# The S5 scan on VectorE alone with real and imaginary state tiles, and short convolutions on padded rows, in a hybrid S5 / SSD / DeltaNet step

## The chip, the core and the metric

The kernel runs on one NeuronCore of a Trainium2 chip. Five engines work side by side: TensorE (PE, with its weight loads shown as PEld), VectorE (DVE), ScalarE (ACT), GpSimd (POOL) and SyncE (SP), which here issues the transfers. Each engine runs its own instructions in a fixed order and waits on semaphores for the others. The metric is the device time of one execution in microseconds; smaller is better.

## What is computed

One layer of an inference step over T = 384 tokens, of which 128 are context and 256 latent (four grid rows of 64). The layer is a SwiGLU block, a mixer with three branches, and a second SwiGLU block; the change is in the mixer.

```python
u_s5, z, xbc, dt_raw, qkv, ... = jnp.split(h @ p['w_in'], IN_SPLITS, axis=-1)
# S5, diagonal complex recurrence, 32 groups x 64 states, forward and backward
y_f, ... = _s5_scan(u, ...);  y_b, ... = _s5_scan(_rev(u), ...)      # h_t = lb * h_{t-1} + B u_t
# short depthwise convolution of width 3, before SSD and DeltaNet
xbc = silu(_short_conv(xbc, ssd_conv_w, grid) + ssd_conv_b)
qkv = silu(_short_conv(qkv, dn_conv_w, grid))
# in _short_conv: context is one sequence of 128 tokens, latent rows are 64 tokens with zero ends
y = xp[:, :, 0:width] * w[0] + xp[:, :, 1:1+width] * w[1] + xp[:, :, 2:2+width] * w[2]
out = (sigmoid(gates) * branches).sum() @ w_out
```

## The kernel before

Tokens lie along the free axis, channels on the 128 partitions. Every dense product is made of three fp32r matmuls (`mm3`, L288): high part of the weight by high part of the input (L291), high by low (L292), low by high (L293). A block of 128 output channels gets its weights in `split_w` (L279): SP transfers 128x1024 numbers to `wraw` (three buffers, L281), ScalarE rounds them to `whi` (L284), VectorE subtracts to `wlo` (L285); `whi` and `wlo` have two buffers. So ScalarE and VectorE both stand between a transfer and TensorE, once for each block, in the order of their own queues.

The mixer comes at about 340 to 620 us. Its order of work is: four blocks of S5 input, the small scalars, twelve convolved blocks for k, q and v (L782 to L793; each q block also starts two `chunk_inputs`, L764, which copy a product from PSUM into the S5 state tile), the S5 scan (L806 to L822), four convolved x blocks, B and C (L830 to L836), the z blocks (L861 to L873), the decay masks (`segments`, L840: POOL makes `Atri`, TensorE sums it, ScalarE takes the exponential), the DeltaNet matrices and their inverse, and the S5 output matmuls (L967), which read the entering states `Hc`.

The order in which an engine's instructions stand is not the order of the source: a scheduler of the framework simulates the program and lays each engine's queue from its own estimates. So conv steps, scan steps and weight splits are interleaved in VectorE's queue, and TensorE's queue mixes z, segments, S5 outputs and further dense blocks.

**The scan.** Each chunk of 8 tokens is one step for 48 chunks; context (16 chunks) and the first half of the latent chain run abreast, so 31 steps do it: 15 of them with two columns (`nx` = 2) and 16 with one. The states are in `Ss[q]`, one tile for 16 of the 32 groups, with real and imaginary part inside. In a step each half takes two products (L818), a sum (L820) and an addition into the state (L822); half 0 is on VectorE, half 1 on GpSimd. When both halves are done ScalarE copies them, shifted by one chunk, into `Hc[q]` (L941 to L943), and GpSimd fills the start columns (L946, L947).

**The convolution** (`conv`, L662, called 18 times). ScalarE copies the block from PSUM to `ur` (L667), VectorE makes the middle tap (L671) and adds two side taps, each in one piece for context (127 columns, L677) and one for latent (4 rows of 63, L679); ScalarE applies SiLU (L681).

## Time and profile before

| | us |
|---|---|
| median of three runs | 1169.02 |
| lowest and highest of them | 1168.38, 1170.4 |
| the profiled execution | 1170.72 |
| its span in the trace | 1168.9 |

| engine | busy in the span |
|---|---|
| PE | 94% |
| PEld | 89% |
| DVE | 69% |
| ACT | 39% |
| POOL | 17% |

TensorE is busy nearly all the time, and its granted clock is 0.974 on average. The shares are averages over the whole span; in the mixer they are different, and the rows below are taken from there. A row of the stages gives the length of a stretch, then the busy time of each engine with its number of instructions, then the granted TensorE clock (1.00 is 2.4 GHz, 0.5 is 1.2 GHz), the DMA share and the bandwidth. A row by line gives line, engine, operation, what is written from what with the shapes, how often, busy time and mean duration, and the idle time of the engine before these instructions with what ended it.

### The profile page before, as it was taken

Reading aid. Unit: us, or ns where it says so; the run is one execution under the profiler, and the core shown is the slowest. Engines: PE = TensorE matmul, PEld = TensorE weight load, DVE = VectorE, ACT = ScalarE, POOL = GpSimd, SP = SyncE. Lnnn points to the kernel's source line nnn. Section 1 sums busy time; section 2 is a strip of 40 time slices with the busy share of each in tenths; the row PEclk is TensorE's granted clock in tenths of the full one; section 3 lists DMA queues with packets and bytes.
Section 4 is the critical chain, followed back from the end, with each engine's and each line's share of the span. In section 5 each row is a group of like instructions: output and inputs, shape, how many; then the busy total and the mean of one; then the engine's idle time right before and its main releaser. Section 6 shows DMA issues by size and latency. Waiting matters only on the chain.

```text
span 1168.9 us, 19259 instructions
## 1 busy us (share of the span) xinstructions
PE 1104.1 (94%) x7264; PEld 1039.9 (89%) x7264; DVE 807.4 (69%) x1698; ACT 458.0 (39%) x774; POOL 200.3 (17%) x270
## 2 busy tenths in 40 slices
...
GB/s 355 266 265 213 224 212 234 167 167 161 225 167 145 123 164 112 75 124 245 207 138 216 153 120 125 130 201 163 226 195 145 201 130 122 142 126 127 104 124 80
DMA packets 107342, 199.21 MB, mean 170 GB/s; under 512 B 35056, under 2 KB 61936, under 8 KB 106992
## 3 DMA queue, kind: packets, MB, share of 16 engines
...
q14 instruction: 37, 0.30, 0.1%
...
## 4 chain that ended last, share of the span: by engine, by line
PE 75%; DVE 12%; DMA 4%; issue 3%; ACT 3%; POOL 2%; SPq 1%; DVEq 0%; ACTq 0%; POOLq 0%
PE ps_d L293 20%; PE ps_d L291 20%; PE ps_d L292 20%; DVE wlo L285 2%; ACT whi L284 1%; DVE sc L818 1%; DMA wraw<-in_win_dram 1%; PE ps_c L1032 1%; PE ps_d L243 1%; PE ps_s L770 1%; PE ps_m L221 1%; PE ps_s L1032 1%; PE ps_m L849 1%; DVE cv L679 1%; DVE Ss L822 1%
## 5 line engine op out<-in xcount | busy, mean ns | idle before, releaser
L284 ACT CAST whi<-wraw 128x1024 fp32r<-128x1024 f32 (+3 forms) x247 | 227.9, 924 | 466.9 <-PE ps_d L292 306.4
L285 DVE TENSOR_TENSOR wlo<-wraw,whi 128x1024 fp32r<-128x1024 f32 (+3 forms) x247 | 276.3, 1119 | 120.8 <-ACT whi L284 119.7
L291 PE MATMUL ps_d<-hh,whi 128*128 128x384 f32 x696 | 243.1, 350 | 16.2 <-ACT whi L284 13.2
L293 PE MATMUL ps_d<-hh,wlo 128*128 128x384 f32 x696 | 243.7, 351 | 5.5 <-DVE wlo L285 5.4
L292 PE MATMUL ps_d<-hl,whi 128*128 128x384 f32 x696 | 242.2, 348 | 0.6 <-DVE hl L379 0.6
L291 PEld LDWEIGHTS ps_d<-hh,whi 128*128 128x128 f32 x696 | 134.4, 193 | 25.9 <-ACT whi L284 16.8
L293 PEld LDWEIGHTS ps_d<-hh,wlo 128*128 128x128 f32 x696 | 135.0, 194 | 12.8 <-DVE wlo L285 9.7
L292 PEld LDWEIGHTS ps_d<-hl,whi 128*128 128x128 f32 x696 | 135.1, 194 | 3.3 <-issue 1.8
L291 PE MATMUL ps_d<-xh,whi 128*128 128x386 f32 x352 | 120.0, 341 | 0.0
L293 PE MATMUL ps_d<-gh,wlo 128*128 128x384 f32 x352 | 119.1, 338 | 1.0 <-DVE wlo L285 1.0
L293 PE MATMUL ps_d<-xh,wlo 128*128 128x386 f32 x352 | 119.9, 341 | 0.0
L291 PE MATMUL ps_d<-gh,whi 128*128 128x384 f32 x352 | 118.8, 337 | 0.4 <-ACT whi L284 0.4
L292 PE MATMUL ps_d<-xl,whi 128*128 128x386 f32 x352 | 118.9, 338 | 0.0
L292 PE MATMUL ps_d<-gl,whi 128*128 128x384 f32 x352 | 118.6, 337 | 0.0
L271 DVE SCALAR_TENSOR_TENSOR ajunk<-araw,cb 128x1024 bf16<-128x1024 f32 x64 | 77.8, 1215 | 1.6 <-ACT cb L263 1.6
L293 PEld LDWEIGHTS ps_d<-gh,wlo 128*128 128x128 f32 x352 | 66.0, 188 | 2.0 <-DVE wlo L285 1.6
L291 PEld LDWEIGHTS ps_d<-gh,whi 128*128 128x128 f32 x352 | 66.1, 188 | 0.9 <-ACT whi L284 0.7
L292 PEld LDWEIGHTS ps_d<-xl,whi 128*128 128x128 f32 x352 | 66.6, 189 | 0.0
L293 PEld LDWEIGHTS ps_d<-xh,wlo 128*128 128x128 f32 x352 | 66.2, 188 | 0.2 <-DVE wlo L285 0.2
L291 PEld LDWEIGHTS ps_d<-xh,whi 128*128 128x128 f32 x352 | 66.3, 188 | 0.0
L292 PEld LDWEIGHTS ps_d<-gl,whi 128*128 128x128 f32 x352 | 66.1, 188 | 0.0
L431 DVE SCALAR_TENSOR_TENSOR x<-ps_d,gate,x 128x128 f32<-128x128 f32 x64 | 23.7, 412 | 29.3 <-PE ps_d L293 29.3
...
## 6 DMA issues: line engine op xcount, KB each, us to landing
...
```

What stands on the lines that cost most here:

```text
L221: PE.matmul(pt[32 * g:32 * g + 32, :], c32[:, k, :], raw[:, j, :], start=q < 2, stop=q >= 2, tile_position=(0, 32 * g))
L243: PE.matmul(pt[32 * g:32 * g + 32, :], c32[:, 4 * h + g, :], raw[:, g, :], start=h == 0, stop=h == 1, tile_position=(0, 32 * g))
L271: V.scalar_tensor_tensor(junk, raw, 1.0, cb[:, e], op0=ALU.mult, op1=ALU.mult, accum_out=t[:, b, e:e + 1])
L284: S.copy(hi, raw)
L285: V.tensor_tensor(lo, raw, hi.bitcast(F32), op=ALU.subtract)
L291: PE.matmul(pt, hi[:, k, :], xh[k0 + k], start=start and k == 0, stop=False)
L292: PE.matmul(pt, hi[:, k, :], xl[k0 + k], start=False, stop=False)
L293: PE.matmul(pt, lo[:, k, :], xh[k0 + k], start=False, stop=stop and k == nk - 1)
L431: last = V.scalar_tensor_tensor(xv[m][:, s0:s1], py[:, s0:s1], gate[:, m, e:e + 1], xv[m][:, s0:s1], op0=ALU.mult, op1=ALU.add)
L679: V.scalar_tensor_tensor(ol, il, ws, ol, op0=ALU.mult, op1=ALU.add)
L770: PE.matmul(pt[:, ri, g], sw[:, ri, g], UU[:, 4 * b + g], start=True, stop=True)
L1032: PE.matmul(dst[r_, h], lh[r_, h], rh[r_, h] if len(rh.shape) == 3 else rh[r_], start=True, stop=True)
```

## The change

The scan runs on VectorE only, one loop over all 32 groups. `Ss` and `Hc` are split by real and imaginary part and no longer by groups, so a step has two products, one sum and two state additions. `hfin` and `Hc` are copied for each part; all start columns are written by ScalarE. `chunk_inputs` makes its copies for each part, six and no longer three. The convolution has two standing tiles with a zero column at both ends of each of six rows of 64 (two context, four latent): ScalarE copies the block into the middle of the rows, makes the middle tap from PSUM in a second pass, and copies one column each way across the seam of the two context rows; VectorE adds two side taps over all six rows at once.

```diff
@@ -659,24 +659,26 @@
         S.activation(E.rearrange("p a b c d -> p (a b c d)"), pe.rearrange("p a b c d -> p (a b c d)"), AF.Exp)
         return sp, da, beta, E
-    def conv(wk, t2, pt, blk, bias, dst=None, rb=None):
+    def conv(wk, ur, pt, blk, bias, dst=None, rb=None):
         w = sv["cw"][:, blk, :]
-        ur = t2("ur", None)[:, 0:T]
+        rows = lambda v: v.rearrange("p (r c) -> p r c", c=64)
+        mid = ur[:, :, 1:65]
+        cv = wk.tile([P, T], F32, name="cv", tag="sgate", bufs=NSG)
         if rb is None:
-            S.copy(ur, pt)
+            S.copy(mid, rows(pt))
+            S.activation(cv, pt, AF.Identity, scale=w[:, 1:2])
         else:
-            unscaled(ur, pt, rb)
-        cv = wk.tile([P, T], F32, name="cv", tag="sgate", bufs=NSG)
-        V.tensor_scalar(cv, ur, w[:, 1:2], None, op0=ALU.mult)
-        lat_i = ur[:, TC:T].rearrange("p (r c) -> p r c", c=64)
-        lat_o = cv[:, TC:T].rearrange("p (r c) -> p r c", c=64)
-        for tap, (o0, o1, i0, i1) in ((0, (1, None, 0, -1)), (2, (0, -1, 1, None))):
-            ws = w[:, tap:tap + 1]
-            oc, ic = cv[:, 0:TC][:, o0:o1], ur[:, 0:TC][:, i0:i1]
-            V.scalar_tensor_tensor(oc, ic, ws, oc, op0=ALU.mult, op1=ALU.add)
-            ol, il = lat_o[:, :, o0:o1], lat_i[:, :, i0:i1]
-            V.scalar_tensor_tensor(ol, il, ws, ol, op0=ALU.mult, op1=ALU.add)
...
+            S.activation(rows(cv), mid, AF.Identity, scale=w[:, 1:2])
+        S.copy(ur[:, 0, 65:66], ur[:, 1, 1:2])
+        S.copy(ur[:, 1, 0:1], ur[:, 0, 64:65])
+        for tap in (0, 2):
+            V.scalar_tensor_tensor(rows(cv), ur[:, :, tap:tap + 64], w[:, tap:tap + 1], rows(cv), op0=ALU.mult, op1=ALU.add)
         dst = cv if dst is None else dst
         S.activation(dst, cv, AF.Silu, bias=bias if bias is not None else 0.0)
         return dst
@@ -727,6 +729,12 @@
                         live.remove(g)
                     else:
                         yield
+        pads = [mp.tile([P, 6, 66], F32, name=f"ur{n}") for n in range(2)]
+        for t in pads:
+            for c in (0, 65):
+                V.memset(t[:, :, c:c + 1], 0.0)
+        urs = (pads[n % 2] for n in range(18))
         X3 = [slice(x * P, x * P + P) for x in range(3)]
         H2 = [slice(0, 64), slice(64, P)]
@@ -759,7 +767,7 @@
         du = dU.rearrange("(g i) s c -> s i g c", i=16)
         for s in range(8):
             nc.sync.dma_start(out=UU[16 * s:16 * s + 16], in_=du[s])
-        Ss = [big("Ss", (2, 16, 48)) for q in range(2)]
+        Ss = [big("Ss", (32, 48)) for ri in range(2)]
         def chunk_inputs(b):
             sw = w4("sw")
@@ -768,10 +776,11 @@
             for ri in range(2):
                 for g in range(4):
                     PE.matmul(pt[:, ri, g], sw[:, ri, g], UU[:, 4 * b + g], start=True, stop=True)
-            dst = Ss[b // 4][:, :, 4 * (b % 4):4 * (b % 4) + 4]
-            S.copy(dst[0:64], pt[0:64])
-            S.copy(dst[64:128, :, :, 0:16], pt[64:128, :, :, 15::-1])
-            S.copy(dst[64:128, :, :, 16:48], pt[64:128, :, :, 47:15:-1])
+            for ri in range(2):
+                dst = Ss[ri][:, 4 * b:4 * b + 4]
+                S.copy(dst[0:64], pt[0:64, ri])
+                S.copy(dst[64:128, :, 0:16], pt[64:128, ri, :, 15::-1])
+                S.copy(dst[64:128, :, 16:48], pt[64:128, ri, :, 47:15:-1])
         ktok, vtok = big("ktok", (3, 4, P)), big("vtok", (3, 4, P))
@@ -780,9 +789,9 @@
         for which, tokt in ((1, ktok), (0, qtok), (2, vtok)):
             for m in range(4):
...
                 else:
-                    raw = conv(wk, t2, dense_in(10 + 4 * which + m, hh, hl), 6 + 4 * which + m, None)
+                    raw = conv(wk, next(urs), dense_in(10 + 4 * which + m, hh, hl), 6 + 4 * which + m, None)
                 pt = transposes([raw[:, X3[x]] for x in range(3)])
                 S.copy(tokt[:, :, m], pt)
                 if which < 2:
@@ -810,30 +819,28 @@
             nx = 2 if 0 < j < 16 else 1
             cur = slice(x0, x0 + 17, 16) if nx == 2 else slice(x0, x0 + 1)
             prv = slice(x0 - 1, x0 + 16, 16) if nx == 2 else slice(x0 - 1, x0)
-            for q, eng in enumerate((V, G)):
-                gs = slice(16 * q, 16 * q + 16)
-                t = [wk.tile([P, 2, 2, 16], F32, name=f"sc{q}{w}", tag=f"sc{q}{w}", bufs=2) for w in range(2)]
-                for w in range(2):
-                    hv = sv["s5h"][:, w:w + 1, gs] if j == 0 else Ss[q][:, w, :, prv].rearrange("p g x -> p x g")
-                    eng.tensor_tensor(t[w][:, 0:nx], bc(mu[:, w, :, gs], [P, nx, 2, 16], 1),
-                                      bc(hv, [P, nx, 2, 16], 2), op=ALU.mult)
-                eng.tensor_tensor(t[0][:, 0:nx], t[0][:, 0:nx], t[1][:, 0:nx], op=ALU.add)
-                sv_ = Ss[q][:, :, :, cur].rearrange("p r g x -> p x r g")
-                eng.tensor_tensor(sv_, sv_, t[0][:, 0:nx], op=ALU.add)
+            t = [wk.tile([P, 2, 2, 32], F32, name=f"sc{w}", tag=f"sc{w}", bufs=2) for w in range(2)]
+            for w in range(2):
+                hv = sv["s5h"][:, w:w + 1, :] if j == 0 else Ss[w][:, :, prv].rearrange("p g x -> p x g")
+                V.tensor_tensor(t[w][:, 0:nx], bc(mu[:, w], [P, nx, 2, 32], 1), bc(hv, [P, nx, 2, 32], 2), op=ALU.mult)
+            V.tensor_tensor(t[0][:, 0:nx], t[0][:, 0:nx], t[1][:, 0:nx], op=ALU.add)
+            for ri in range(2):
+                sv_ = Ss[ri][:, :, cur].rearrange("p g x -> p x g")
+                V.tensor_tensor(sv_, sv_, t[0][:, 0:nx, ri], op=ALU.add)
         hfin = mp.tile([P, 2, 32], F32, name="hfin")
-        for q in range(2):
-            S.copy(hfin[:, :, 16 * q:16 * q + 16], Ss[q][:, :, :, 15])
+        for ri in range(2):
+            S.copy(hfin[:, ri], Ss[ri][:, :, 15])
         nc.sync.dma_start(out=o["s5"], in_=hfin)
         xtok = mp.tile([P, 3, 8, 64], F32, name="xtok")
         for m in range(4):
-            raw = conv(wk, t2, dense_in(4 + m, hh, hl), m, sv["cb"][:, m:m + 1])
+            raw = conv(wk, next(urs), dense_in(4 + m, hh, hl), m, sv["cb"][:, m:m + 1])
             pt = transposes([raw[:, X3[x]] for x in range(3)])
             S.copy(xtok.rearrange("p x h c -> p x (h c)")[:, :, m * P:m * P + P], pt)
         bT, cT = mp.tile([P, T], F32, name="bT"), mp.tile([P, T], F32, name="cT")
-        conv(wk, t2, dense_in(8, hh, hl), 4, sv["cb"][:, 4:5], bT)
-        conv(wk, t2, dense_in(9, hh, hl), 5, sv["cb"][:, 5:6], cT)
+        conv(wk, next(urs), dense_in(8, hh, hl), 4, sv["cb"][:, 4:5], bT)
+        conv(wk, next(urs), dense_in(9, hh, hl), 5, sv["cb"][:, 5:6], cT)
         btok = mp.tile([P, 3, P], F32, name="btok")
         S.copy(btok, transposes([bT[:, X3[x]] for x in range(3)]))
@@ -936,15 +943,16 @@
         Hc = []
-        for q in range(2):
-            hc = big("Hc", (2, 16, 48))
-            S.copy(hc[0:64, :, :, 1:48], Ss[q][0:64, :, :, 0:47])
-            S.copy(hc[64:128, :, :, 0:15], Ss[q][64:128, :, :, 14::-1])
-            S.copy(hc[64:128, :, :, 16:47], Ss[q][64:128, :, :, 46:15:-1])
-            h0 = sv["s5h"][:, :, 16 * q:16 * q + 16]
+        for ri in range(2):
+            hc = big("Hc", (32, 48))
+            h0 = sv["s5h"][:, ri]
             for r_, z0, i0 in ((H2[0], 0, 16), (H2[1], 15, 47)):
-                G.memset(hc[r_, :, :, z0:z0 + 1], 0.0)
-                G.tensor_copy(hc[r_, :, :, i0], h0[r_])
+                S.activation(hc[r_, :, z0], ones[r_, 0:32], AF.Copy, scale=0.0)
+                S.copy(hc[r_, :, i0], h0[r_])
+            S.copy(hc[0:64, :, 1:16], Ss[ri][0:64, :, 0:15])
+            S.copy(hc[0:64, :, 17:48], Ss[ri][0:64, :, 16:47])
+            S.copy(hc[64:128, :, 0:15], Ss[ri][64:128, :, 14::-1])
+            S.copy(hc[64:128, :, 16:47], Ss[ri][64:128, :, 46:15:-1])
             Hc.append(hc)
         gsh, gsl = blocks("gsh", 4, FR), blocks("gsl", 4, FR)
@@ -962,7 +970,7 @@
                 G4 = 2 * j + g
                 for n in range(3):
                     for q in range(2):
-                        lh = UU[:, 16 * q + G4] if n == 0 else Hc[q][:, n - 1, G4]
+                        lh = UU[:, 16 * q + G4] if n == 0 else Hc[n - 1][:, 16 * q + G4]
                         rh = tw[:, q, 2 * (j % 2) + g] if n == 0 else ew[:, q, n - 1, g]
                         PE.matmul(pt[64 * q:64 * q + 48, 2 * (j % 2) + g], lh, rh, start=n == 0, stop=n == 2)
             if j % 4 == 0:
```

The order of the queues changes with it. On VectorE around a conv of the scan stretch there stand before: weight split, scan step (`sc`, `Ss`) and conv pieces (`cv`).

```order
L285 TENSOR_TENSOR wlo<-wraw,whi 128x1024
L822 TENSOR_TENSOR Ss<-Ss,sc_4659 128x2x32
L671 TENSOR_SCALAR cv<-ur,smalls_95 128x384
L818 TENSOR_TENSOR sc_4671<-mu,Ss 128x64
L818 TENSOR_TENSOR sc_4672<-mu,Ss 128x64
L677 SCALAR_TENSOR_TENSOR cv<-ur,smalls_95,cv 128x127
L679 SCALAR_TENSOR_TENSOR cv<-ur,smalls_95,cv 128x4x63
L820 TENSOR_TENSOR sc_4671<-sc_4671,sc_4672 128x64
L677 SCALAR_TENSOR_TENSOR cv<-ur,smalls_95,cv 128x127
L679 SCALAR_TENSOR_TENSOR cv<-ur,smalls_95,cv 128x4x63
L822 TENSOR_TENSOR Ss<-Ss,sc_4671 128x2x32
```

And after the change, with the scan steps over all groups:

```order
L825 TENSOR_TENSOR sc_4614<-mu,Ss 128x128
L825 TENSOR_TENSOR sc_4615<-mu,Ss 128x128
L826 TENSOR_TENSOR sc_4614<-sc_4614,sc_4615 128x128
L681 SCALAR_TENSOR_TENSOR cv<-ur_3418,smalls_95,cv 128x384
L829 TENSOR_TENSOR Ss<-Ss,sc_4614 128x2x32 x2
L681 SCALAR_TENSOR_TENSOR cv<-ur_3418,smalls_95,cv 128x384
L825 TENSOR_TENSOR sc_4621<-mu,Ss 128x64
L825 TENSOR_TENSOR sc_4622<-mu,Ss 128x64
L826 TENSOR_TENSOR sc_4621<-sc_4621,sc_4622 128x64
L285 TENSOR_TENSOR wlo<-wraw,whi 128x1024
L829 TENSOR_TENSOR Ss<-Ss,sc_4621 128x32 x2
L681 SCALAR_TENSOR_TENSOR cv<-ur_3419,smalls_95,cv 128x384
```

A two-column step has five instructions of twice the width and no longer four, and a conv has two and no longer five between them.

On ScalarE, in the stretch in which the q blocks are convolved and the chunk products are copied (`Ss<-ps_s`), there stand before:

```order
L284 CAST whi<-wraw 128x1024
L667 COPY ur<-ps_d 128x384
L772 COPY Ss<-ps_s 64x2x192
L773 COPY Ss<-ps_s 64x2x4x16
L774 COPY Ss<-ps_s 64x2x4x32
L772 COPY Ss<-ps_s 64x2x192
L773 COPY Ss<-ps_s 64x2x4x16
L774 COPY Ss<-ps_s 64x2x4x32
```

And after, where L670 and L671 are the copy and the middle tap of a conv and L678, L679 the seam columns:

```order
L683 ACTIVATE cv<-cv 128x384
L670 COPY ur_3418<-ps_d 128x6x64
L781 COPY Ss<-ps_s 64x192
L782 COPY Ss<-ps_s 64x4x16
L783 COPY Ss<-ps_s 64x4x32
L781 COPY Ss<-ps_s 64x192
L782 COPY Ss<-ps_s 64x4x16
L783 COPY Ss<-ps_s 64x4x32
L678 COPY ur_3418<-ur_3418 128x1
L679 COPY ur_3418<-ur_3418 128x1
L683 ACTIVATE cv<-cv 128x384
L796 COPY qtok<-ps_m 128x3x128
```

Two chunk products are now twelve copies, and between a conv's copy (L670) and its seam columns (L678), which VectorE's first side tap needs, six of them stand here.

On TensorE, at the first S5 output matmul that reads `Hc`, there stand before (L869 to L871 are z, L849 the masks, L901 and L902 DeltaNet products):

```order
L871 MATMUL ps_d<-wlo,hh 128x256
L869 MATMUL ps_d<-whi,hh 128x256
L870 MATMUL ps_d<-whi,hl 128x256
L687 MATMUL ps_m<-ident,bT 128x128 x3
L871 MATMUL ps_d<-wlo,hh 128x256
L849 MATMUL ps_m<-Atri,strict 128x512 x4
L967 MATMUL ps_s<-ew,Hc 48x128
L901 MATMUL ps_m<-kT 128x128
```

And after:

```order
L291 MATMUL ps_d<-hh,whi 128x384
L292 MATMUL ps_d<-hl,whi 128x384
L293 MATMUL ps_d<-hh,wlo 128x384
L291 MATMUL ps_d<-hh,whi 128x384
L975 MATMUL ps_s<-ew,Hc 48x128 x2
L908 MATMUL ps_m<-kT 128x128
L909 MATMUL ps_m<-qT,kT 128x128
```

Before, the first of these matmuls stands alone in the middle of z, with 72 matmuls of z behind it, and the next eleven right behind z. Now the first stands behind the whole of z and four mask sums, with 46 matmuls of two further dense blocks (L291 to L293) and eight small ones between. In GpSimd's queue the scan rows are gone, and the masks follow each other directly.

## Rows read from the trace of the kernel before

**Rows 1.** From the first part of the page: engine, busy us, share, instructions.

```profile
PE 1104.1 (94%) x7264; PEld 1039.9 (89%) x7264; DVE 807.4 (69%) x1698; ACT 458.0 (39%) x774; POOL 200.3 (17%) x270
```

**Rows 2.** Stages: length, busy us of each engine, granted clock, DMA share, GB/s.

```profile
390.00:438.00 48.00, 48.00 (x325) 47.80 (x324) 32.86 (x89) 34.07 (x70) 0.02 (x1) 1.00 0.44 141
438.00:500.00 62.00, 51.06 (x313) 47.94 (x311) 59.91 (x158) 27.56 (x47) 54.64 (x118) 0.97 0.33 98
500.00:515.00 15.00, 13.30 (x92) 12.90 (x93) 6.90 (x21) 8.38 (x12) 12.86 (x28) 0.78 0.30 89
515.00:540.00 25.00, 25.00 (x219) 22.43 (x218) 12.84 (x37) 7.25 (x12) 13.31 (x12) 1.00 0.79 231
540.00:590.00 50.00, 38.85 (x315) 32.70 (x313) 25.07 (x81) 16.73 (x31) 14.35 (x14) 0.83 0.74 208
```

**Rows 3.** Waits of PE in 425 to 530: total us, times, longest.

```profile
PE ps_s L967 <- POOL Hc L947: 5.4, 1, 5.4
```

**Rows 4.** Chain of waits in 425 to 530: start us, us, what.

```profile
501.70 0.66 PE ps_s L967 x2
...
514.78 0.96 PE ps_m L849 x4
```

**Rows 5.** VectorE by line, 438 to 500: busy us, mean ns, idle before.

```profile
L818 DVE TENSOR_TENSOR sc<-mu,Ss 128x32 f32<-128x32 f32 (+1 forms) x48 | 14.2, 335 | 0.4
L285 DVE TENSOR_TENSOR wlo<-wraw,whi 128x1024 fp32r<-128x1024 f32 x10 | 12.8, 1284 | 0.0
L679 DVE SCALAR_TENSOR_TENSOR cv<-ur,smalls,cv 128x252 f32<-128x252 f32 x17 | 9.1, 535 | 0.0
L677 DVE SCALAR_TENSOR_TENSOR cv<-ur,smalls,cv 128x127 f32<-128x127 f32 x16 | 7.8, 490 | 0.0
L820 DVE TENSOR_TENSOR sc<-sc,sc 128x32 f32<-128x32 f32 (+1 forms) x24 | 7.4, 308 | 0.4
L822 DVE TENSOR_TENSOR Ss<-Ss,sc 128x32 f32<-128x32 f32 (+1 forms) x24 | 7.2, 301 | 0.4
L803 DVE TENSOR_TENSOR ktok<-ktok,rqk 128x512 f32<-128x512 f32 x3 | 3.6, 1241 | 0.0
L671 DVE TENSOR_SCALAR cv<-ur,smalls 128x384 f32<-128x384 f32 x8 | 3.4, 423 | 0.0
```

**Rows 6.** VectorE in order of time: start us, us, instruction.

```profile
430.88 0.44 DVE L818 TENSOR_TENSOR sc<-mu,Ss 128x64 f32<-128x64 f32 x2
...
431.93 0.46 DVE L818 TENSOR_TENSOR sc<-mu,Ss 128x64 f32<-128x64 f32 x2
...
473.57 0.35 DVE L818 TENSOR_TENSOR sc<-mu,Ss 128x32 f32<-128x32 f32 x2
...
474.44 0.40 DVE L818 TENSOR_TENSOR sc<-mu,Ss 128x32 f32<-128x32 f32 x2
```

**Rows 7.** VectorE by line and shape, whole span.

```profile
L1275 DVE SCALAR_TENSOR_TENSOR mab<-re,ps_d 128x384 f32<-128x384 f32 x8 | 4.4, 552 | 5.6 <-PE ps_d L293 5.6
...
L463 DVE TENSOR_TENSOR pw<-pw 128x128 f32<-128x128 f32 x1 | 0.3, 280 | 0.0
```

**Rows 8.** GpSimd beside VectorE in order of time.

```profile
485.29 3.15 POOL L847 TENSOR_TENSOR Atri<-smalls,dahl 128x512 fp32r<-128x512 f32 x3
...
485.46 2.05 DVE L818 TENSOR_TENSOR sc<-mu,Ss 128x32 f32<-128x32 f32 x2
```

**Rows 9.** ScalarE by line, 390 to 438.

```profile
L667 ACT COPY ur<-ps_d 128x384 f32<-128x384 f32 x8 | 3.9, 483 | 0.0
L772 ACT COPY Ss<-ps_s 64x384 f32<-64x384 f32 x8 | 3.8, 472 | 4.7 <-PE ps_s L770 4.6
...
L773 ACT COPY Ss<-ps_s 64x128 f32<-64x128 f32 x8 | 2.1, 261 | 0.1
```

**Rows 10.** ScalarE by line, 495 to 520.

```profile
L941 ACT COPY Hc<-Ss 64x1504 f32<-64x1504 f32 x2 | 2.9, 1452 | 1.3 <-DVE Ss L822 1.1 <-POOL Ss L822 0.2
...
L943 ACT COPY Hc<-Ss 64x992 f32<-64x992 f32 x2 | 2.0, 1020 | 0.0
```

6 lines of the change are left out of this document (5 added, 1 removed).

## The prediction

> **What bounds the kernel now.** I began with the shares of the page: TensorE is busy 94% of the span [rows 1], so a change in another engine's work can only give back time in which TensorE stands or runs at a low clock. I then cut the mixer into stages [rows 2]. The reader is to see three things there. From 390 to 438 us TensorE is busy without a gap, and ScalarE is busy 34.07 of 48 us. From 438 to 500 TensorE is busy 51.06 of 62 us while VectorE is busy 59.91: VectorE is the bound, and GpSimd beside it is busy 54.64. From 500 to 515 TensorE is short by 1.70 us and its clock is 0.78, between its two levels, after the idle time ahead of it. So 10.94 + 1.70 = 12.6 us of standing TensorE, and about 0.22 x 13.3 = 2.9 us and 0.03 x 51 = 1.5 us of low clock, 17 us in all, belong to the stretch that the change touches. The 11.2 idle us from 540 to 590 are another matter: there the DMA share is 0.74.
>
> Next I asked what TensorE waits for. The longest wait is for `Hc` from GpSimd, 5.4 us, ending at 501.70 [rows 3, 4]; the last masks of z's stretch end the next part at 514.78 [rows 4]. What fills VectorE in 438 to 500 is seen by line [rows 5]: scan products 14.2, sums 7.4, state additions 7.2, conv pieces 9.1 + 7.8 + 3.4, ten weight splits 12.8, `ktok` 3.6. These sum to 65.5, more than the busy time, since the ends of one instruction lie under the next.
>
> **The change, part by part.**
>
> *Convolutions.* On VectorE a conv costs now 2 x 0.535 + 2 x 0.490 + 0.423 = 2.47 us of durations [rows 5]. After, it is two additions over 128x384. The nearest row is an addition of that shape at 552 ns [rows 7], with one operand in another memory, so 1.1 us. It saves 1.37 us each, 11 us over the eight convs of 438 to 500, at the 59.91/65.5 = 0.91 us of queue per us of duration about 10 us. It all lies on the bound of that stretch. The price is on ScalarE: a second pass over 384 columns like the copy at 483 ns, and two copies of one column. From 483 ns at 384 columns and 261 at 128 [rows 9] a copy costs about 150 ns + 0.87 ns a column, so 0.48 + 2 x 0.15 = 0.78 us each.
>
> *Scan.* Before, half the groups cost VectorE a step of 1.05 us with two columns (430.88 to 431.93) and 0.87 with one (473.57 to 474.44) [rows 6]. A full step has three instructions of twice the width and one more addition. At 128x128 a VectorE operation took 280 ns [rows 7]; at half of that width the pair of products took 0.44, so 0.22 each. Three instructions grow by 0.06, and the fifth adds between 0.12 (only its issue) and 0.28 (its whole duration). A step is then 1.35 to 1.5, and with one column 1.0 to 1.15. With other work lying between the dependent instructions, as the order shows, the waits for the previous result are hidden; then a step is little more than its issue, and the old periods, 0.95 and 0.87, are the lower end. Over 15 + 16 steps: 28 us at the low end, 41 at the high one. I take 34, nearer to the measured periods, since in part of the steps nothing lies between.
>
> When does it end? Before, VectorE could start its half early; GpSimd's, with the later chunk products, began at 438 (0.02 us busy before it, 54.64 behind) [rows 2]. Now the loop needs all groups, so it begins there. From then VectorE has: scan 34; eight convs at 1.0, 8; twelve weight splits (the queue after has twelve within the scan) at 1.2, 14.4; `ktok` without a scan beside it 3 x 0.7, 2.1; of the 6.90 + 12.84 us of z and DeltaNet work that stood in 500 to 540 [rows 2] about 7 that the order now puts inside. That is 65.5. Beside GpSimd's masks something is lost: with three mask products in 3.15 us on GpSimd, a pair of scan products took 2.05 us instead of 0.35 [rows 6, 8], 1.7 of 3.15. About eight such products of 1.05 us now stand beside the scan: 4.5 us, of which half a us may fall into waits anyway, 4. The scan ends at 507.5; with its two ends, 501 to 515.
>
> *`Hc`.* ScalarE's copies after the scan: two long ones of the real part and eight of the imaginary. The 1020 ns at 992 columns and 1452 at 1504 [rows 10] give 0.84 ns a column, so 1.02 x 2 for the first; for the second 1.02 x 2 + 0.59 x 2 + 4 x 0.2 = 4.0. `Hc` is whole 6.1 us after the scan, at 513.6.
>
> *What TensorE does meanwhile.* In the new order it needs `Hc` only after all of z, four mask sums, and 46 matmuls of two further blocks. In the stretch 390 to 438 it took 48/325 = 0.148 us a matmul, so those 46 are 6.8 us, with eight small ones about 7.5. In the kernel before, the same point of progress (four mask sums from 514.78, 0.96 us [rows 4], and this 7.5) is reached at about 523.2. If nothing stalled, TensorE would be there 12.6 + 4.4 = 17 us earlier, at 506.2; I leave 2 us of waits for weight splits and 1.5 for ScalarE (below), 509.7. So `Hc` at 513.6 decides, and the gain is 9.6 us. The masks, which GpSimd now makes at once, let the DeltaNet products begin sooner and fill some of the wait; for that I add 1 and take 10.5.
>
> *ScalarE from 390 to 438.* Eight convs x 0.78 = 6.2. The chunk copies: six instead of three for each of eight products, same columns in total, three more fixed costs of 0.15, so 0.45 x 8 = 3.6. That makes 34.07 + 9.8 = 43.9 of 48 us. It fits, with 4 us of slack in place of 13.9; TensorE, which has no gap there, would lose what does not fit. I take 1.5, between 0 and 10. A conv's first side tap waits for the seam columns, and these stand behind six chunk copies on ScalarE; while VectorE waits for them, scan steps and weight splits are queued behind it. Before the scan VectorE has 48 - 32.86 = 15 us of slack, so that costs nothing there.
>
> *Nothing for:* the zero columns of the standing tiles (once, long before), the output copy of the final state (behind TensorE's path), and the 8 start columns of `Hc` that were GpSimd's.
>
> *A rule that bears on it.* The row of the masks shows 54% of GpSimd's time lost to VectorE [rows 8]. The Trainium skill (SBUF — State Buffer, section "Who interferes with whom") says that VectorE and GpSimd share one pair of ports under an exclusive lock, and that the loser is blocked for the whole instruction. By this rule in full the eight products would cost 8.4 us and not 4.5. It speaks for taking the scan off GpSimd, and against a scan that stands on VectorE alone beside GpSimd's masks; what it does to the end is the late scan below.
>
> **The sum.** 1170.72 of the profiled execution - 10.5 = 1160.2. That execution lies 1.7 above the median, 1169.02, so the median after is put at 1158.5. Its own range: with the scan at 28 us `Hc` comes at 507.6 and is no limit, and without the 3.5 us left for waits the gain is 17; with the scan at 41 us it is 10.5 - 7 = 3.5. That is 1152 to 1165.5.
>
> **Rivals.**
>
> *The late scan.* The steps show their whole latency, 41 us, and the masks block VectorE for their whole length, 8.4 us, not 4. The scan ends at 507.5 + 7 + 4.4 = 519, `Hc` comes at 525, and TensorE has by then used up the two extra blocks and stands: the gain is 523.2 - 525, none. For it: one engine has both halves in series, and each step is a chain of results that wait for one another. Against: in the row 54% are lost, and in the order other work lies in most steps. Time 1166 to 1172.
>
> *ScalarE becomes the bound, and the kernel is slower.* The place is 390 to 438. The point from which it decides is whether its idle time there, 13.9 us, is slack or is bound to arrivals (products that come late, taps that it must wait for). If all of it stays, 48 + 9.8 us pushes every weight rounding, and with it TensorE and the scan's start, back by 9.8; and in 438 to 500 each of eight taps stands 0.5 us for its seam columns at the head of VectorE's queue, 4 us more. Then -10.5 + 9.8 + 4 = +3.3, 1172.3. For it: ScalarE makes every `whi`, and in its queue six chunk copies stand between a conv's copy and its seams. Against: its busy share there is 71%.
>
> *More than that.* With GpSimd free, the masks and the DeltaNet chain start some 15 us sooner, and half of the 11.2 idle us and of the 0.17 x 38.9 us of low clock from 540 to 590 goes [rows 2], 5.6 + 3.3 = 9: -10.5 - 9 = -19.5, 1149.5. Against: that stretch hangs on transfers, and the fill blocks that covered it are taken two blocks earlier. The same earlier use of fill, turned round, gives back up to 7 us of the gain there, 1165.5, the far end of the forecast's range.
>
> **How the numbers follow.** The forecast has 0.50, the larger gain 0.14, the late scan 0.20, ScalarE as the bound 0.16. A change of 0.2%, 2.3 us, is about what this measurement can tell. Faster: 0.50 + 0.14 + 0.06 of the late scan = 0.70. Same: 0.08 of the late scan and 0.03 of ScalarE's, 0.11. Slower: 0.06 + 0.13 = 0.19. The range takes in the forecast, the far part of the larger gain's, and the late scan, and leaves out most of ScalarE's: 1147 to 1171.
>
> **What would show it.** Right: VectorE's state additions end at 502 to 513; a full step of 0.95 to 1.4 us; two side taps of about 0.55; TensorE's longest wait at the S5 output below 3 us, and TensorE busy over 57 of 62 us in 438 to 500 at a clock of 1.00. Wrong: idle TensorE in 390 to 438 behind `whi`; VectorE waiting for ScalarE at the side taps inside the scan; the last state addition after 516 with TensorE waiting for ScalarE's `Hc`; more than 15 idle us of TensorE in the 50 us after, where now 11.2 stand.

## The result

The changed kernel took 1157.81 us in the median of five runs (1153.03 to 1162.95), beside 1169.02 us for the kernel before. The ratio is 0.9899, 95% interval 0.9872 to 0.9925: about 11 us faster. In a second series it took 1161.64 against 1169.69, ratio 0.9928 (0.9906 to 0.995), 8 us. The forecast was 1158.5.

The profile of the changed kernel, by the stages of [rows 2]:

```profile
390.00:438.00 48.00, 48.00 (x323) 47.82 (x322) 29.64 (x58) 41.15 (x120) 4.40 (x4) 1.00 0.51 154
438.00:500.00 62.00, 57.19 (x382) 53.42 (x381) 60.67 (x180) 34.03 (x75) 9.23 (x9) 1.00 0.35 101
500.00:515.00 15.00, 14.58 (x129) 11.16 (x127) 9.42 (x27) 10.28 (x18) 7.72 (x8) 1.00 0.63 199
515.00:540.00 25.00, 22.45 (x190) 19.92 (x186) 10.07 (x30) 9.12 (x16) 5.99 (x6) 1.00 0.86 239
540.00:590.00 50.00, 41.72 (x337) 36.04 (x333) 26.19 (x84) 15.74 (x28) 17.45 (x15) 0.90 0.83 231
```

From 438 to 500 TensorE is busy 57.19 us, not 51.06, at full clock; from 500 to 515 it is at 1.00 instead of 0.78. VectorE is as full as before, 60.67 us, and GpSimd has fallen from 54.64 to 9.23. What TensorE waits for from 425 to 530 answers to [rows 3]:

```profile
PE ps_m L856 <- DVE Lo L916: 1.4, 1, 1.4
PE ps_d L878 <- DVE wlo L285: 1.4, 2, 1.1
PE ps_d L293 <- DVE wlo L285: 1.1, 2, 0.7
...
PE ps_s L975 <- ACT Hc L955: 0.4, 1, 0.4
```

The 5.4 us for `Hc` have become 0.4. VectorE in 438 to 500, answering to [rows 5]:

```profile
L825 DVE TENSOR_TENSOR sc<-mu,Ss 128x128 f32<-128x128 f32 (+1 forms) x56 | 20.2, 401 | 0.0
...
L829 DVE TENSOR_TENSOR Ss<-Ss,sc 128x64 f32<-128x64 f32 (+1 forms) x54 | 12.2, 273 | 0.6
L681 DVE SCALAR_TENSOR_TENSOR cv<-ur,smalls,cv 128x384 f32<-128x384 f32 x16 | 9.9, 620 | 0.0
```

A side tap is 0.62 us and there are two to a conv, a state addition 0.27. The last addition began at 504.4:

```profile
L829 DVE TENSOR_TENSOR Ss<-Ss,sc x62: 200/260/1084, 431.6 to 504.4; 128x32 f32<-128x32 f32 x32, 128x64 f32<-128x64 f32 x30
```

A good part of one profile's lead can be chance, though. The profiled run, 1153.03 us, lies at the lower end of its series, 17.7 us below the profiled run of before, and 6 us of that are there by 390 us, where the changed work has only begun (its first side tap starts at 383.6): TensorE stands some us between 360 and 380, in both kernels, and in the kernel before it ran the next ten us at half clock. Here are 380 to 390 us of before, of the changed kernel, and of the changed kernel when it was run and profiled again (in each: busy times of TensorE, its weight loads, VectorE, ScalarE, GpSimd; then the granted clock):

```profile
380.00:390.00 10.00, 10.00 (x41) 10.00 (x41) 6.32 (x17) 2.75 (x4) 0.00 (x0) 0.51 0.43 147
```

```profile
380.00:390.00 10.00, 10.00 (x68) 9.95 (x68) 8.90 (x12) 7.68 (x16) 5.61 (x4) 1.00 0.59 211
```

```profile
380.00:390.00 10.00, 10.00 (x41) 10.00 (x41) 6.91 (x11) 4.06 (x10) 3.80 (x3) 0.55 0.49 174
```

The same program had 1.00 (2.4 GHz) once and 0.55, mostly 1.2 GHz, the other time, with 7.37 + 9.48 us and 7.71 + 7.17 us of TensorE work in the twenty us ahead of it. So below, kernels are compared by medians and ratios, and where two profiles are compared it is with the second one (span 1161.0, 7.9 below that of before).

How much further TensorE is can be counted from the traces, by the columns of all matmuls begun (both kernels have 2,233,328 in the span, where a matmul of fewer than 64 columns is counted as 64): for a moment of the kernel before, the lead is how much earlier the other kernel had as many columns. The second profile of the changed kernel is level with before at 438 (0.5 us behind), 3.1 us ahead at 470, 5.1 at 490, 10.3 at 500, 14.6 at 510, 8.9 at 530, and 7.7 ahead at 1000. So all of the gain is won from 438 to 510, and 6 us of it are handed back right behind that.

### The profile page after: what moved, and what is told of

The parts are those of the page before. It is cut to its first block, busy times and chain, and to the rows that moved or that the text cites. A ratio compares the mean times of both kernels' runs of the same rounds, so it can differ in the third digit from the quotient of the medians.

```text
span 1151.2 us, 19217 instructions
## 1 busy us (share of the span) xinstructions
PE 1097.4 (95%) x7264; PEld 1029.8 (89%) x7264; DVE 798.4 (69%) x1679; ACT 475.3 (41%) x862; POOL 150.8 (13%) x138
## 4 chain that ended last, share of the span: by engine, by line
PE 78%; DVE 9%; DMA 4%; issue 3%; ACT 3%; SPq 2%; POOL 1%; DVEq 0%; POOLq 0%; ACTq 0%
PE ps_d L291 21%; PE ps_d L293 21%; PE ps_d L292 21%; DVE wlo L285 3%; ACT whi L284 1%; PE ps_s L778 1%; DMA wraw<-in_win_dram 1%; DVE sc L825 1%; PE ps_c L1040 1%; PE ps_d L243 1%; PE ps_m L856 1%; PE ps_s L1040 1%; DVE Ss L829 1%; DMA ew<-dE 1%; PE ps_m L221 1%
## 5 line engine op out<-in xcount | busy, mean ns | idle before, releaser
L291 PE MATMUL ps_d<-hh,whi 128*128 128x384 f32 x696 | 241.1, 348 | 14.8 <-ACT whi L284 12.2
L293 PE MATMUL ps_d<-hh,wlo 128*128 128x384 f32 x696 | 241.5, 348 | 3.8 <-DVE wlo L285 3.7
L291 PEld LDWEIGHTS ps_d<-hh,whi 128*128 128x128 f32 x696 | 133.3, 192 | 25.0 <-ACT whi L284 16.2
L293 PEld LDWEIGHTS ps_d<-hh,wlo 128*128 128x128 f32 x696 | 133.2, 191 | 10.8 <-DVE wlo L285 7.8
L291 PE MATMUL ps_d<-xh,whi 128*128 128x386 f32 x352 | 120.0, 341 | 0.0
L293 PE MATMUL ps_d<-xh,wlo 128*128 128x386 f32 x352 | 119.9, 341 | 0.0
L293 PE MATMUL ps_d<-gh,wlo 128*128 128x384 f32 x352 | 119.1, 338 | 0.6 <-DVE hdng L1290 0.4
L291 PE MATMUL ps_d<-gh,whi 128*128 128x384 f32 x352 | 118.8, 337 | 0.4 <-ACT whi L284 0.4
L293 PEld LDWEIGHTS ps_d<-gh,wlo 128*128 128x128 f32 x352 | 66.0, 188 | 1.7 <-DVE hdng L1290 0.7
L291 PEld LDWEIGHTS ps_d<-gh,whi 128*128 128x128 f32 x352 | 66.1, 188 | 0.9 <-ACT whi L284 0.7
L293 PEld LDWEIGHTS ps_d<-xh,wlo 128*128 128x128 f32 x352 | 66.2, 188 | 0.2 <-DVE wlo L285 0.2
L291 PEld LDWEIGHTS ps_d<-xh,whi 128*128 128x128 f32 x352 | 66.3, 188 | 0.0
L854 POOL TENSOR_TENSOR Atri<-smalls,dahl 128x512 fp32r<-128x512 f32 x36 | 40.9, 1150 | 85.0 <-DVE dahl L762 73.1
```

The source lines that it names most:

```text
L291: PE.matmul(pt, hi[:, k, :], xh[k0 + k], start=start and k == 0, stop=False)
L293: PE.matmul(pt, lo[:, k, :], xh[k0 + k], start=False, stop=stop and k == nk - 1)
L854: G.tensor_tensor(A, bc(INCL[d], [P, 4, P], 1), bc(dahl[:, w, x, 12 * d + c0:12 * d + c0 + 4], [P, 4, P], 2), op=ALU.mult)
```

## The experiments

Each kernel was timed against the kernel before on the same chip; "after" is the changed kernel here, and a time "above after" is above the 1161.64 us of the second series. Experiments 1 to 4, 5 to 8 and 9 to 12 are three series, whose medians for the kernel before lie within 0.6 us. The theories: A, VectorE's queue and GpSimd's half of the scan bound the stretch together, and the gain needs both parts of the change; B, the convolutions alone made it; C, it is the spared half clock; D, taking the scan off GpSimd made it, since the two engines hold each other up; E, it is the new place of the `Hc` matmuls in TensorE's queue.

**1. The convolutions alone.** The new `conv` in the kernel before; scan, chunk copies and `Hc` as they were.

> The kernel before with only the new convolutions: padded rows, ScalarE making the middle tap and the seam columns, VectorE two side taps. Scan, chunk copies and Hc as before, half of the groups on GpSimd. Theory A (VectorE's queue and GpSimd's half of the scan bound 438 to 500 together; the gain needs both parts of the change): VectorE is relieved by about 10 us, the weight splits come earlier, but GpSimd's last state addition stays at about 505 to 509, and with it the masks behind it and the wait for Hc: 1163 us, minus 4 to minus 8. Theory B (the convolutions alone made the gain, the scan's move is neutral): 1158, minus 10 to minus 12. Theory C (the gain of the changed kernel is mostly the clock stretch at 380 to 390 us that happened to be spared): 1168.

Measured: 1173.59 us against 1169.69, ratio 1.003 (1.0014 to 1.0045): slower, where all three theories had said faster or nothing. The stretch 438 to 500 and its two longest waits of TensorE:

```profile
438.00:500.00 62.00, 51.14 (x284) 48.78 (x282) 45.65 (x112) 32.56 (x73) 54.90 (x127) 0.86 0.28 86
```

```profile
PE ps_s L975 <- POOL Hc L955: 4.4, 1, 4.4
PE ps_m L689 <- ACT qT L813: 3.0, 1, 3.0
```

VectorE is busy 14 us less (45.65 instead of 59.91), of which 9 are the conv pieces (11.3 us instead of the 20.3 of [rows 5]), about the 10 of the forecast; for the rest it stands, 6.5 us for weight roundings and 7.2 for z's first step on ScalarE. TensorE gained nothing: it is busy 51.14 us, at a clock of 0.86 instead of 0.97. It now waits for GpSimd's queue, where half of the scan still takes until 499.6:

```profile
L830 POOL TENSOR_TENSOR Ss<-Ss,sc x31: 268/356/1363, 436.1 to 499.6; 128x32 f32<-128x32 f32 x16, 128x64 f32<-128x64 f32 x15
```

`qT` needs a scaling that stands between GpSimd's scan steps. Theory A's mechanism is there (GpSimd's half is the next bound, right behind VectorE), but its size was wrong, and B falls.

**2. The scan alone.** The scan's part of the change with the old `conv`.

> The kernel before with only the scan's part of the change: one loop on VectorE over all groups, real and imaginary tiles, six chunk copies, Hc by parts; convolutions as before. Theory A: VectorE carries 10 us more of conv pieces than in the changed kernel between the scan's start and end, so the scan ends at about 515 instead of 504.7, Hc comes at 521, TensorE stands for it about 5 to 8 us: 1169, between minus 3 and plus 3. Theory B: 1169 too. Theory D (the move off GpSimd itself is the gain, since the two engines no longer hold each other up): 1161, minus 6 to minus 10.

Measured: 1174.52 against 1169.69, ratio 1.005 (1.003 to 1.007).

```profile
438.00:500.00 62.00, 52.64 (x341) 49.28 (x339) 61.38 (x168) 28.62 (x53) 19.35 (x14) 1.00 0.34 102
500.00:515.00 15.00, 13.97 (x92) 13.70 (x92) 14.24 (x41) 4.02 (x7) 6.14 (x7) 0.89 0.31 88
515.00:540.00 25.00, 21.52 (x166) 18.70 (x165) 19.64 (x59) 12.13 (x21) 8.32 (x9) 0.93 0.57 176
```

```profile
PE ps_d L868 <- DVE zt L858: 4.7, 1, 4.7
PE ps_d L291 <- DVE zt L858: 2.0, 1, 2.0
```

```profile
L821 DVE TENSOR_TENSOR Ss<-Ss,sc x62: 199/264/1126, 436.6 to 527.4; 128x32 f32<-128x32 f32 x32, 128x64 f32<-128x64 f32 x30
```

GpSimd is free of the scan, VectorE is full from 438 to 527.4, and TensorE stands for z's last step on VectorE in 515 to 540 (21.52 of 25 us; 25.00 before). By matmul columns this kernel is 12.1 us ahead at 500 and 1.7 us ahead at 530. D falls: taking the scan off GpSimd wins nothing by itself.

**3. Two halves on VectorE.** The new `conv`, and the old scan with both halves on VectorE:

```diff
-            for q, eng in enumerate((V, G)):
+            for q, eng in enumerate((V, V)):
```

> The new convolutions, and the scan as before by halves of the groups, but with both halves on VectorE: eight instructions of half width a step instead of five of full width; chunk copies and Hc as before. Theory A (the length of the scan on VectorE decides when Hc comes): 31 steps of about 1.5 to 1.6 us of VectorE instead of about 1.1, 12 to 15 us later than in the changed kernel, of which TensorE's further blocks cover some: 1166 to 1170, 8 to 12 above the changed kernel. Rival (merging does not matter, taking the scan off GpSimd does): within 3 us of the changed kernel, 1155 to 1161.

Measured: 1162.87 against 1169.69, ratio 0.995 (0.9928 to 0.9971), that is 1.2 us above after in the same series. The scan did not end later but 8.8 us earlier:

```profile
L830 DVE TENSOR_TENSOR Ss<-Ss,sc x62: 204/262/1134, 424.7 to 502.7; 128x32 f32<-128x32 f32 x32, 128x64 f32<-128x64 f32 x30
```

Here the rival was right: merging the halves into wide instructions, and the tiles by real and imaginary part that go with it, are not where the gain is. Merging does spare VectorE work: from 420 to 505 the scan's instructions take 24.5 + 15.6 + 12.7 = 52.8 us by line,

```profile
L826 DVE TENSOR_TENSOR sc<-mu,Ss 128x64 f32<-128x64 f32 (+1 forms) x120 | 24.5, 258 | 0.3
L830 DVE TENSOR_TENSOR Ss<-Ss,sc 128x32 f32<-128x32 f32 (+1 forms) x62 | 15.6, 276 | 1.0 <-ACT Ss L782 0.7
...
L828 DVE TENSOR_TENSOR sc<-sc,sc 128x64 f32<-128x64 f32 (+1 forms) x60 | 12.7, 233 | 0.3
```

and in the second profile of after 21.4 + 13.8 + 8.4 = 43.6 us. But the first half can begin at 424.7, before all chunk products are there, 13.9 us earlier than the scan of that profile.

**4. The changed kernel again.**

> The changed kernel once more, with a profile of its own. Theory A: 1155 to 1160 us, and in the profile the weight splits lead those of before by some 5 us at 390 to 430 only if the clock stays at its full level between 380 and 390; the lead of some 12 us won between 434 and 515 is there in either case. Theory C: without that stretch of full clock the lead shrinks to below 6 us and the time is above 1163.

Measured: 1161.64 us, ratio 0.9928, with the half clock at 380 to 390 shown above. The lead won between 434 and 515 is there without it: the weight split that starts at 434.4 in before starts 1.2 us later here, and the one at 514.1 starts 11.0 us earlier. The stretch explains most of the 8.9 us of columns between the two profiles of one program (5.5 us of it are there by 390), and C no part of the 7.9 us between the second profile and that of before, which had the stretch at half clock as well. Which clock the other runs of the two kernels had there is not known.

**5. GpSimd relieved, convolutions alone.** As experiment 1, with the q scaling on VectorE and the start columns of `Hc` on ScalarE:

```diff
-                eng = V if which else G
+                eng = V
...
-                G.memset(hc[r_, :, :, z0:z0 + 1], 0.0)
-                G.tensor_copy(hc[r_, :, :, i0], h0[r_])
+                S.activation(hc[r_, :, :, z0], bc(ones[r_, 0:16], [64, 2, 16], 1), AF.Copy, scale=0.0)
+                S.copy(hc[r_, :, :, i0], h0[r_])
```

> The convolutions alone, as in the run of the convolutions alone (1173.6 us), but with GpSimd relieved of all but its half of the scan and the masks there: the q scaling on VectorE and the start columns of Hc on ScalarE. Theory A (with VectorE relieved, GpSimd's own queue became what TensorE waits for: 3.0 us for qT, whose scaling stands between GpSimd's scan steps, and 4.4 us for Hc, whose start columns stand behind the last step): those waits go or halve, 1166 to 1170. Rival (the loss of the convolutions alone comes from ScalarE's extra work, or from the order behind 540 us): 1172 to 1175.

Measured: 1178.24 against 1169.11, ratio 1.007 (1.0042 to 1.0099). The wait for `Hc` went and 0.7 us of that for `qT` were left, and others came:

```profile
PE ps_d L877 <- ACT cv L671: 6.9, 1, 6.9
PE ps_m L689 <- ACT kT L813: 3.6, 1, 3.6
```

A z block waited 6.9 us for ScalarE's middle tap, for that second pass reads the product from PSUM and holds its buffer until it has run. The tap ran at 496.90, since it stood in ScalarE's queue behind the copies into `Hc`, and these waited 5.67 us for the last step of GpSimd's half:

```profile
493.90 1.44 ACT L949 COPY Hc<-Ss 64x1504 f32<-64x1504 f32 x1 [5.67 <-POOL Ss L830]
```

So GpSimd's half is still what TensorE waits for, now by way of ScalarE, and the cause given in experiment 1 was not the whole one: the first copy had read the product by 488.2, so the second reading of PSUM is a price of the new `conv` that the forecast had left out. In after the same wait is absent from the list of 425 to 530.

**6. A dearer scan.** After, with the second product of each step computed twice.

> The changed kernel with the second product of each scan step computed twice: 31 more VectorE instructions of about 0.3 us on the chain, 8 to 10 us. Theory A (VectorE's scan still sets when Hc is ready and TensorE comes there with little to spare): the last state addition 8 to 10 us later, TensorE waits for Hc, 5 to 9 us above the changed kernel, 1166 to 1170. Rival (what bounds now is the transfers from 540 on, so the end of the scan has slack): less than 2 above, 1160 to 1163.

Measured: 1174.93 against 1169.11, ratio 1.0045 (1.0027 to 1.0063), 13 us above after.

```profile
L830 DVE TENSOR_TENSOR Ss<-Ss,sc x62: 201/264/1105, 437.5 to 536.8; 128x32 f32<-128x32 f32 x32, 128x64 f32<-128x64 f32 x30
```

```profile
PE ps_d L293 <- DVE wlo L285: 6.9, 7, 2.2
PE ps_s L976 <- DMA tw<-dK: 6.3, 2, 4.2
...
PE ps_s L976 <- ACT Hc L956: 3.0, 1, 3.0
```

The added products took 12.4 us by line (30 of 0.41 us) and not 8 to 10, and the scan ended 25 us later, since the scheduler also laid other work between the steps (15 weight splits instead of 12). TensorE waits again for `Hc`, for weight splits, and then for the transfers of the S5 output stage. So after is on the edge: 12.4 us more of VectorE's queue cost 13.

**7. The middle tap back on VectorE.**

```diff
-            S.activation(cv, pt, AF.Identity, scale=w[:, 1:2])
+            V.tensor_scalar(rows(cv), mid, w[:, 1:2], None, op0=ALU.mult)
```

> The changed kernel with the middle tap back on VectorE, from the padded rows, instead of ScalarE's second pass. Theory A: eight middle taps of 0.42 us lie inside the scan, 3.3 us on VectorE's queue, and ScalarE gives back about 0.5 us each from 390 to 438, of which little counts: 1 to 3 us above the changed kernel, 1162 to 1165. Rival (ScalarE's load from 390 to 438 costs more than VectorE's queue): 1 to 3 below, 1158 to 1160.

Measured: 1170.64 (1162.46 to 1173.53) against 1169.11, ratio 1.0003 (0.9981 to 1.0025): the whole gain is gone, 9 us for the 3.3 us that A had counted. Its profile shows where a part of it lies, from 438 to 540:

```profile
PE ps_d L291 <- DVE zt L866: 3.6, 1, 3.6
PE ps_d L876 <- DVE zt L866: 2.9, 2, 1.7
```

TensorE stands 6.5 us for z's step on VectorE. The profiled run lies at the lower end of a wide series (span 1161.9), and it had the full clock from 380 to 390, as the first profile of after had (1.00 in both); beside that one it is 10.7 us longer. By columns it is some 2 us behind it at 500 and 7 to 8 at 515: from 505 to 510 TensorE is busy 1.44 of 5 us, and its clock is 0.56 and 0.76 in the two stretches of 5 us that follow.

**8. Both scalings on ScalarE.**

```diff
-                eng = V if which else G
-                eng.tensor_tensor(tokt[:, x], tokt[:, x], bc(rq[:, which, x], [P, 4, P], 2), op=ALU.mult)
+                for m in range(4):
+                    S.activation(tokt[:, x, m], tokt[:, x, m], AF.Identity, scale=rq[:, which, x, m:m + 1])
```

> The changed kernel with the scaling of k and q on ScalarE (24 instructions of 128 columns with a scale per channel row) instead of three each of 512 columns on VectorE and GpSimd. Theory A: VectorE loses 3.6 us of work inside the scan, GpSimd 4.3 us of work beside it, ScalarE has the room after 438: the scan ends 3 to 5 us earlier and the time is 1 to 4 us below the changed kernel, 1157 to 1160. Rival (the end of the scan has slack): within 1 us of it; or ScalarE's 7 us hold up the weight roundings: 1 to 3 above.

Measured: 1165.26 against 1169.11, ratio 0.996 (0.994 to 0.998), 3.6 above after.

```profile
L829 DVE TENSOR_TENSOR Ss<-Ss,sc x62: 202/223/291, 437.3 to 490.3; 128x32 f32<-128x32 f32 x32, 128x64 f32<-128x64 f32 x30
```

```profile
438.00:500.00 62.00, 56.67 (x366) 54.08 (x365) 54.76 (x186) 47.63 (x113) 3.00 (x3) 0.94 0.37 108
```

The last state addition begins at 490.3 instead of 511.5, and TensorE is not helped: with ScalarE at 47.63 us it waits 3.5 us for a weight rounding, and is busy 56.67 us, where the second profile of after has 59.31.

**9. Only the place of the Hc matmuls.** The kernel before, with `Hc` tied to the end of z:

```diff
-                G.memset(hc[r_, :, :, z0:z0 + 1], 0.0)
+                S.activation(hc[r_, :, :, z0], zt[r_, 0:32].rearrange("p (a b) -> p a b", b=16), AF.Copy, scale=0.0)
```

> The kernel before, with one edit: the zero column of Hc is made by ScalarE from the last z tile (times zero), so that Hc exists only after z and the scheduler puts every S5 output matmul behind z, the masks and about 34 matmuls of further blocks, as it did in the changed kernel. Theory A (the gain is VectorE's and GpSimd's relief; the order follows from it): the 5.4 us wait in the middle of z goes, but the weight splits of z still come out of a full VectorE queue and GpSimd's masks still stand behind its scan, so 2 to 5 us below before, 1164 to 1167. Rival E (the gain is mostly the place of the Hc matmuls in TensorE's queue): 8 to 11 below, 1158 to 1161.

Measured: 1170.51 against 1169.61, ratio 1.0009 (0.9996 to 1.0021).

```profile
438.00:500.00 62.00, 51.41 (x305) 48.54 (x303) 58.03 (x147) 28.93 (x48) 52.72 (x118) 0.92 0.31 94
```

With the `Hc` matmuls behind z, as in after (the first stands at 519.5), and the scan and convolutions of before, TensorE is busy 51.41 us in 438 to 500, about the 51.06 of [rows 2]. The wait of 5.4 us is gone from the list and its time is filled by others (4.1 us for `btok` the longest). E falls.

**10. GpSimd's company.** After, with GpSimd computing half of the scan's products into a tile that is not read:

```diff
+                gt_ = wk.tile([P, 2, 2, 16], F32, name=f"gs{w}", tag="gs", bufs=1)
+                G.tensor_tensor(gt_[:, 0:nx], bc(mu[:, w, :, 0:16], [P, nx, 2, 16], 1),
+                                bc(hv[:, :, 0:16], [P, nx, 2, 16], 2), op=ALU.mult)
```

> The changed kernel with GpSimd made to compute the two products of each scan step for half of the groups as well, into a tile that nobody reads: 62 GpSimd instructions of about 0.4 us beside VectorE's scan, and no result to wait for. Theory A (part of the gain is that the two engines no longer hold each other up): VectorE's scan instructions get longer, the scan ends 5 to 10 us later, 3 to 8 us above the changed kernel, 1164 to 1170. Rival (only GpSimd's place on the chain counted, not its company): within 2 us of the changed kernel, 1159 to 1163.

Measured: 1160.95 against 1169.61, ratio 0.9927 (0.9902 to 0.9952), level with after. VectorE's products from 430 to 520, in this kernel and in after:

```profile
L825 DVE TENSOR_TENSOR sc<-mu,Ss 128x128 f32<-128x128 f32 (+1 forms) x60 | 23.4, 424 | 0.0
```

```profile
L825 DVE TENSOR_TENSOR sc<-mu,Ss 128x128 f32<-128x128 f32 (+1 forms) x60 | 21.4, 393 | 0.0
```

```profile
L827 POOL TENSOR_TENSOR gs<-mu,Ss 128x64 f32<-128x64 f32 (+1 forms) x60 | 31.7, 528 | 74.7 <-DVE rsq L308 45.7 <-DVE Ss L832 26.5 <-DVE rsq L307 0.3
```

With 31.7 us of GpSimd work beside it a product takes 0.424 instead of 0.393 us and the scan 76.2 instead of 73.0 us. The two engines do hold each other up, and with products as short as these it costs no time that the runs can tell.

**11. The q scaling on VectorE.** The line of experiment 5 in after.

> The changed kernel with the q scaling on VectorE too, so that k's and q's six scalings run there without GpSimd beside them. By the row of an uncontended operation of that width, 0.69 us, six cost 4.1 us where three cost 3.6 beside GpSimd. Theory A: the same queue on VectorE, qT earlier, the time within 2 us of the changed kernel, 1159 to 1163. Rival (VectorE's queue is so tight that each us added costs more): 3 to 6 above.

Measured: 1163.01 against 1169.61, ratio 0.994 (0.9921 to 0.9959), 1.4 above after: level.

**12. Halves and scalings on VectorE.** Experiment 3 with that line.

> Both halves of the scan on VectorE in the old tiles, with the new convolutions and both scalings on VectorE: the run of the two halves ended its scan 9 us earlier than the changed kernel (502.9 against 511.7) and this takes GpSimd's scalings from its side. Theory A (that end has little left to give, TensorE's wait for Hc was 0.4 us): 1160 to 1165, level with the changed kernel. Rival (an earlier end of the scan goes on paying): 1154 to 1158.

Measured: 1163.41 against 1169.61, ratio 0.9939 (0.9915 to 0.9963): level with experiments 3 and 11. The scan ended 8 us earlier than in after and nothing came of it.

No kernel here is faster than the changed one by more than the intervals tell.

## Why the prediction was right

**The sum.** -10.5 was forecast, -11.2 and -8.1 were measured; that the first series comes within 0.7 us of the forecast is partly luck, for the second lies 3.1 above it. The mechanism, TensorE's standing and low clock from 438 to 515 given back by a shorter VectorE queue and a free GpSimd, is what the traces show, and only both parts together bring it: +3.9 for the convolutions, +4.8 for the scan, -8.1 for both in one series. The forecast treated the parts as terms that add up, the convolutions at 10 us of queue and the scan's move as a cost; alone, each was a loss.

**Scan.** The start was forecast at 438 and the end at 507.5, 69.5 us; both profiles show 73.0 (431.6 to 504.6 and 438.6 to 511.6). I had taken 34 us for the steps, thinking that other work hides the waits between dependent instructions. Where steps stand alone they come every 1.43 us with two columns and every 1.0 with one (486.80 to 487.81 in the second profile); with two, as in 458.12 to 459.57 here:

```profile
458.12 0.71 DVE L825 TENSOR_TENSOR sc<-mu,Ss 128x128 f32<-128x128 f32 x2
458.86 0.29 DVE L826 TENSOR_TENSOR sc<-sc,sc 128x128 f32<-128x128 f32 x1
459.19 0.46 DVE L829 TENSOR_TENSOR Ss<-Ss,sc 128x64 f32<-128x64 f32 x2
459.57 0.68 DVE L825 TENSOR_TENSOR sc<-mu,Ss 128x128 f32<-128x128 f32 x2
```

That makes 15 x 1.43 + 16 x 1.0 = 37 us, nearer to the upper end than to the lower. By line the scan took 43.6 us (experiment 3), of which 5.1 are time lost to GpSimd's long instructions (below). The lower end, 28, was itself a slip: it set 0.95 for a period of two columns that [rows 6] show at 1.05. `ktok`, put at 2.1 us, took 3.6 (3 x 1.24) beside GpSimd's scaling of q; in experiment 11, with both scalings on VectorE, it took 3 x 0.69.

**Convolutions.** Two taps of 0.62 instead of 0.55 us; the saving on VectorE held (experiment 1: conv pieces of 11.3 us instead of 20.3). Its price on ScalarE was set at 0.78 us a conv, all of it work of ScalarE's own; that the second pass keeps a PSUM buffer taken was missed, and shows in experiment 5, where z waits 6.9 us for it while ScalarE itself stood 5.67 us for GpSimd.

**ScalarE.** Forecast 43.9 us busy in 390 to 438 and a loss of 1.5 us. Measured 41.15 and 40.57; by the weight splits of the first profile the lead falls from 6.5 us at 417 to 5.0 at 422, 1.5, and in the second from 1.0 at 417 to 1.2 behind at 434, 2.2. The rows that carry it:

```profile
L671 ACT ACTIVATE cv<-ps_d,smalls 128x384 f32<-128x384 f32 x9 | 5.4, 599 | 0.0
L781 ACT COPY Ss<-ps_s 64x192 f32<-64x192 f32 x16 | 5.0, 312 | 0.5 <-PE ps_s L778 0.4
...
L783 ACT COPY Ss<-ps_s 64x128 f32<-64x128 f32 x16 | 4.2, 260 | 0.0
...
L782 ACT COPY Ss<-ps_s 64x64 f32<-64x64 f32 x16 | 3.3, 208 | 0.2
```

64, 128 and 192 columns take 208, 260 and 312 ns, which is the 150 ns + 0.87 ns a column of the forecast within 2%. The rival of ScalarE as the bound did not come; in experiment 8, which adds 7.4 us to it, TensorE waited 3.5 us for a weight rounding.

**Hc decides.** This step was wrong. `Hc` was forecast 6.1 us after the scan and is whole 6.7 after it (511.3 in the first profile, 518.3 in the second), but TensorE, forecast to be there 3.9 us before, waited 0.4 us in the first profile and not at all in the second: it came there later than I thought, held by `Lo`, weight splits and z's steps on VectorE. A later scan end is dear (experiment 6), an earlier one brought nothing (3, 8, 12). By these waits what decides is VectorE's whole queue up to the end of z, in which the scan is one share; no run shows that by itself. It shows best in the second profile just ahead of the scan's end, where VectorE is busy 4.86 of 5 us and TensorE 2.89:

```profile
500.00:505.00 5.00, 2.89 (x19) 2.16 (x18) 4.86 (x18) 0.53 (x2) 1.48 (x1) 1.00 0.08 26
505.00:510.00 5.00, 5.00 (x22) 4.75 (x23) 4.84 (x16) 1.29 (x2) 1.25 (x2) 0.66 0.72 184
```

With the 0.66 of the next five us, that is where part of the 14.6 us lead of 510 goes. The forecast had the point of progress of 523.2 reached at 513.6; in the second profile the first matmul that reads `Hc` begins at 517.4. But there is more work ahead of it than was put: the 46 matmuls come every 0.17 us and not every 0.148, and 16 of L243 lie among them. By columns the kernel before is as far only at 526.5. So the lead at this place is 9.1 us, near the 9.6 of the forecast, and `Hc` did not set it: that the number came out is luck in this step.

**The rule of the ports.** VectorE's products grow by 8% when GpSimd computes products beside them (experiment 10). That is the direction that the Trainium skill states (SBUF — State Buffer, section "Who interferes with whom"): an instruction of VectorE with two inputs in SBUF contends with one of GpSimd that reads there. Beside GpSimd's long instructions, the 128x512 ones of the masks and the DeltaNet matrices, the loss is far larger. The second profile of after, VectorE's scan and GpSimd:

```profile
492.18 1.20 DVE L829 TENSOR_TENSOR Ss<-Ss,sc 128x32 f32<-128x32 f32 x2
493.31 2.16 DVE L825 TENSOR_TENSOR sc<-mu,Ss 128x64 f32<-128x64 f32 x2
```

```profile
492.16 1.04 POOL L897 TENSOR_TENSOR segb<-seg,nbt 128x512 f32<-128x512 f32 x1 [46.87 <-ACT seg L859]
493.16 1.15 POOL L899 TENSOR_TENSOR segd<-seg,smalls 128x512 f32<-128x512 f32 x1
494.27 1.07 POOL L897 TENSOR_TENSOR segb<-seg,nbt 128x512 f32<-128x512 f32 x1
```

Two state additions take 1.20 us instead of 0.33, and two products 2.16 instead of 0.47: the first addition and the two products end at 493.27, 494.43 and 495.47, each about 0.1 us after the GpSimd instruction beside it (493.20, 494.31, 495.34). That is the whole blocking that the prediction took from the section. Steps on VectorE that read PSUM are not held up: z's takes 0.41 us at 496.38, beside GpSimd's `Atri`, and 0.41 elsewhere. Eight GpSimd instructions, 9.2 us, stand beside this scan, and its instructions are longer by 5.1 us for them, where the forecast had eight, 4.5 us of loss and 4 in the sum. So the term was nearly right, though its row had been misread: the pair of 485.46 [rows 8] stands beside two of the three mask products, not all, and the third held up a conv piece (1.15 us instead of 0.49). In experiment 8 no such GpSimd instruction stands beside the scan, and no state addition takes more than 0.29 us. Taking the short products of the scan off GpSimd is no part of the gain that can be measured; the long instructions cost the scan 5.1 us, and what they cost the kernel no run shows.

**Left open.** Every edit makes the scheduler lay all queues anew, so a run compares two whole orders, not one instruction more or less: 3.3 us of VectorE work cost 9 in experiment 7, and 12 us moved the scan's end by 25 in experiment 6. How much of these, and of the losses of experiments 1 and 2, belongs to the work and how much to the order was not separated; that would need one order with two durations. Of the order only the place of the `Hc` matmuls was tried by itself, in the kernel before, and it won nothing (experiment 9).
